# The last rows of a down projection, once by feature rows with seven-product sums, once by token rows

## The chip, the cores and the metric

The kernel runs on one core of a Trainium2 chip. The metric is the device time of one execution in microseconds (us); smaller is better. The engines are called as in the profile: PE (TensorE), DVE (VectorE), ACT (ScalarE), POOL (GpSimd) and SP (SyncE, which issues nearly all transfers).

## What is computed

One layer of a streaming encoder: norm, attention in two kinds of heads, output projection, residual, norm, SwiGLU FFN, residual, and a last norm. Only the end matters here. `x` has 576 tokens (512 of the prompt, 64 of the sample) of 2048 features; the FFN is 5632 wide.

```python
def rmsnorm(x, g):
    xf = x.astype(jnp.float32)
    y = xf * lax.rsqrt(jnp.mean(xf * xf, axis=-1, keepdims=True) + EPS)
    return (y * g.astype(jnp.float32)).astype(x.dtype)
...
    h = rmsnorm(x, lp['norm_ffn_g'])
    x = x + (jax.nn.silu(h @ lp['ffn_w_gate']) * (h @ lp['ffn_w_up'])) @ lp['ffn_w_down']
...
    y_prompt = rmsnorm(xp[:, N_META:], final_norm_g)
    y_sample = rmsnorm(xs, final_norm_g)
```

## The kernel before, in words

Activations lie with features on the partitions and tokens along the columns: a tile is 128 features x 576 tokens, used in two halves of 288 (`QH`). Every operand of a product is split into a high and a low part in a reduced format (`split`: ACT copies the high part, DVE subtracts it to get the low one), and a product is three matmuls: high x high, low x high, high x low. Nearly all instructions of DVE, ACT and SP are recorded by one helper, so the profile gives them line L125.

**Seven products.** FFN and down projection use `winograd`: four quarters of a 256 x 256 piece of weights and four of the activations are combined so that seven products do the work of eight. A product's weights are a raw quarter or a sum (`subtotal`, on POOL and DVE, tiles `ws`), split into `wh` and `wl`; its activations are the operand tiles `b1` to `b7` of a pair. A **pair** is 256 FFN features (two tiles), numbered `u` or `m`, 22 in all; operand tile `b{p}_{m % 8}` holds product p of pair m.

**FFN.** 44 turns: a gate turn and an up turn for each pair u, 168 matmuls each. The result of a pair is turned into its operands: the four quarters and four sums (POOL, L1770 to 1773), which `parts` splits on ACT and DVE into seven pieces and stores in `partspill` (288 KB each), one piece a step of the following turn. The first two pairs (`WHOLE`) and the last two are stored whole instead (`actspill`, `sumspill`). The last turn (`ending`, up turn of pair 21) already loads the operands of block 0 step by step (`starter`), two steps ahead of their use; whole ones are split in place. From the ending turn on SP's issues stand in program order, and DVE's and ACT's order is set by the scheduler except where `pin` fixes it.

**Down projection.** Blocks of pairs, `blocks = [4, 4, 4, 4, 4, 2]`. For each of the first five, eight passes d (256 output features each): raw weights are loaded (1024 KB), seven products of 12 matmuls follow (L1436 with `wh`, L1440 with `wl`), and `take` adds each product from PSUM to the running sums `y[i]` (16 tiles, features on partitions, residual included). While a block runs, `fetcher` loads the next one's operands from `partspill`, and before the last block `builder` loads and splits the quarters of pairs 20 and 21.

**The last block** (pairs 20 and 21, 512 weight rows) multiplies plainly: `plain_weights` loads and splits, `plain_rows` does mm3 (L193, 3 matmuls for each of 4 k-chunks, 288 columns), and after each, `squares` forms the square of the finished sum (ACT or POOL, L1831, L1836) and scales the sum by the last norm's gain (ACT). First all passes for token half 0, then for half 1. `finish` sums the squares over the partitions by a matmul with ones (L1863), turns the sums to token rows by transposes on PE (L1849, 96 tokens), scales them by the root on the way out of PSUM (DVE and ACT in turn) and stores them (28 stores).

## Time and profile before

| what | value |
|---|---|
| median of 3 runs | 2393.21 us (2392.88 to 2395.0) |
| profiled execution, its own time | 2394.53 us |
| its span, first to last instruction | 2392.8 us |
| mean granted clock of PE | 0.997 |
| PE busy | 2365.2 us, 99% |
| DVE, ACT, POOL busy | 1782.5, 1169.8, 718.0 us |
| last plain product to end of span | 2375.4 to 2392.8 |

The span is what the hardware profiler saw of one execution; the 1.7 us between it and that execution's time lie before the first or after the last instruction. Busy times of different engines overlap. A group of the trace gives the operation as tile written <- tiles read, with the shape; `SPq` is SP's issue of transfers.

### The profile page before, as it was taken

How to read it: one execution, taken by the hardware profiler on the slowest of the kernel's cores; microseconds unless marked ns; L12 is line 12 of the kernel's file. 1: busy time of each engine (PE TensorE's matmuls, PEld its weight loads, DVE VectorE, ACT ScalarE, POOL GpSimd, SP SyncE). 2: the span in 40 equal slices, each digit the busy share in tenths (PEclk: the TensorE clock that was granted, in tenths of full speed). 3: DMA queues.
4: the chain of work that ended last, by engine and by line, in shares of the span. 5: the costliest groups of instructions: out<-in, count | busy, mean ns of one | idle time of the engine just before them, and what ended most of it. 6: DMA issues, size and time to landing. Idle time of an engine off the chain costs nothing.

```text
span 2392.8 us, 44550 instructions
## 1 busy us (share of the span) xinstructions
PE 2365.2 (99%) x17580; PEld 2333.4 (98%) x17580; DVE 1782.5 (74%) x2823; ACT 1169.8 (49%) x2223; POOL 718.0 (30%) x568
## 2 busy tenths in 40 slices
PE   9999999999999999999999999999999999999998
PEld 8999999999999999999999999999999999999998
DVE  5665666676565788788888888888887887888873
ACT  5544445455454554455545555555545433333345
POOL 0000000020001454554454454454454322222223
PEclk9999999999999999999999999999999999999999
DMA  9423323353223553334434434434435964754332
GB/s 276 125 86 86 93 85 94 94 159 113 89 94 114 166 170 108 126 107 154 160 111 151 161 118 143 161 120 141 160 129 175 315 230 143 232 188 140 120 113 80
DMA packets 329266, 336.92 MB, mean 141 GB/s; under 512 B 22482, under 2 KB 273272, under 8 KB 329024
## 3 DMA queue, kind: packets, MB, share of 16 engines
q1 hardware_dynamic: 327520, 330.56, 42.7%
q0 software_dynamic: 1104, 3.22, 0.4%
q8 instruction: 138, 2.26, 0.4%
q14 instruction: 72, 0.59, 0.1%
q10 hardware_dynamic: 432, 0.29, 0.0%
HBM read 264.68 MB, written 72.68 MB: 141 GB/s over the span
## 4 chain that ended last, share of the span: by engine, by line
PE 59%; DVE 1%; DMA 0%; issue 0%; POOL 0%; ACT 0%; DVEq 0%; ACTq 0%; POOLq 0%; SPq 0%
PE m L1436 38%; PE m L1440 19%; PE m L193 2%; PE m L1849 0%; DVE wl L125 0%; DMA raw<-in_ffn_w_down 0%; DVE ws L125 0%; DMA b<-actspill 0%; POOL ws L1396 0%; DVE b L125 0%; PE m L1863 0%; DVE y L125 0%; ACT wh L125 0%; DVEq L2014 0%; DVE c L125 0%
## 5 line engine op out<-in xcount | busy, mean ns | idle before, releaser
L1436 PE MATMUL m<-b,wh 128*128 128x288 f32 x7168 | 1051.9, 296 | 2.7 <-DVE y L125 1.5
L1436 PEld LDWEIGHTS m<-b,wh 128*128 128x128 f32 x7168 | 983.2, 188 | 5.1 <-ACT wh L125 2.4
L1440 PE MATMUL m<-b,wl 128*128 128x288 f32 x3584 | 569.2, 294 | 1.9 <-DVE wl L125 1.8
L1396 POOL TENSOR_TENSOR ws<-raw 128x512 f32<-128x512 f32 (+1 forms) x258 | 364.8, 1423 | 539.6 <-DVE wl L125 277.7
L1440 PEld LDWEIGHTS m<-b,wl 128*128 128x128 f32 x3584 | 509.3, 188 | 3.3 <-DVE wl L125 3.3
L125 ACT ACTIVATE wh<-ws 128x512 fp32r<-128x512 f32 (+1 forms) x339 | 282.8, 845 | 392.0 <-PE m L1436 257.2
L125 DVE TENSOR_TENSOR wl<-ws,wh 128x512 fp32r<-128x512 f32 (+1 forms) x339 | 384.6, 1145 | 91.6 <-ACT wh L125 89.1
L125 DVE TENSOR_TENSOR wl<-raw,wh 128x512 fp32r<-128x512 f32 (+1 forms) x389 | 359.8, 949 | 10.2 <-ACT wh L125 9.6
L125 ACT ACTIVATE wh<-raw 128x512 fp32r<-128x512 f32 (+1 forms) x389 | 228.5, 620 | 283.8 <-PE m L1436 261.5
L108 PE MATMUL ps<-xh,wh 128*128 128x296 f32 (+1 forms) x960 | 217.6, 308 | 1.7 <-ACT wh L125 1.7
L108 PE MATMUL ps<-xl,wh 128*128 128x296 f32 (+1 forms) x960 | 208.5, 298 | 0.1
L125 DVE TENSOR_TENSOR y<-y,m 128x288 f32<-128x288 f32 x312 | 140.1, 450 | 90.0 <-PE m L1440 68.1
L108 PE MATMUL ps<-xh,wl 128*128 128x296 f32 (+1 forms) x928 | 202.1, 299 | 0.5 <-DVE wl L125 0.5
L125 DVE TENSOR_TENSOR ws<-ws,raw 128x512 f32<-128x512 f32 (+1 forms) x129 | 117.9, 920 | 58.5 <-POOL ws L1396 56.4
L108 PEld LDWEIGHTS ps<-xh,wh 128*128 128x128 f32 x960 | 155.4, 190 | 5.5 <-ACT wh L125 2.1
L108 PEld LDWEIGHTS ps<-xl,wh 128*128 128x128 f32 x960 | 155.8, 189 | 0.4 <-DVE xl L125 0.3
L108 PEld LDWEIGHTS ps<-xh,wl 128*128 128x128 f32 x928 | 151.0, 189 | 1.0 <-DVE wl L125 1.0
L125 DVE TENSOR_TENSOR wl<-wr,wh 128x1024 fp32r<-128x1024 f32 (+1 forms) x110 | 114.3, 1041 | 30.4 <-ACT wh L125 28.9
L125 ACT ACTIVATE wh<-wr 128x1024 fp32r<-128x1024 f32 (+1 forms) x112 | 99.8, 893 | 63.0 <-PE ps L108 36.2
L1651 POOL TENSOR_TENSOR c<-c,rb 128x576 f32<-128x576 f32 x42 | 67.2, 1599 | 168.8 <-ACT c L125 168.8
L703 POOL MEMSET bias<- 64x64 f32 x8 | 1.2, 144 | 365.3 <-DMA bias<-tsk 258.6
L1764 POOL TENSOR_TENSOR c<-c 128x576 f32<-128x576 f32 x42 | 73.7, 1754 | 87.3 <-DVE c L125 82.9
(420 smaller groups left out, 3109.0 us busy)
## 6 DMA issues: line engine op xcount, KB each, us to landing
raw<-in_ffn_w_gate SPq DMA_DIRECT2D x44, 1024.0 KB, 5.8
raw<-in_ffn_w_up SPq DMA_DIRECT2D x44, 1024.0 KB, 6.4
raw<-in_ffn_w_down SPq DMA_DIRECT2D x39, 1024.0 KB, 5.6
partspill<-parts SPq DMA_DIRECT2D x126, 288.0 KB, 2.1
b<-partspill SPq DMA_DIRECT2D x126, 288.0 KB, 6.2
wr<-in_w_in SPq DMA_DIRECT2D x54, 512.0 KB, 3.8
wr<-in_w_out SPq DMA_DIRECT2D x16, 512.0 KB, 4.0
wr<-in_w_out SPq DMA_DIRECT2D x28, 256.0 KB, 3.2
```

The source lines that it names most:

```text
L108: self.tc.keep_in_program_order(self.pe.matmul(out, lhsT, rhs, start=start, stop=stop))
L125: ins = issue(*args, **kwargs)
L193: PE.matmul(outs[i], w, x[i], start=start and p == 0, stop=stop and p == 2)
L703: G.memset(bias[0:64, 464:528], -BIG)
L1396: engine.tensor_tensor(w[:, k:k + m, :], pick(xs), pick(ys), op=op)
L1436: PE.matmul(banks[p], wh[:, k, :], x, start=first and new and k == 0 and x is hi, stop=False, skip_group_check=not new)
L1440: PE.matmul(banks[p], wl[:, k, :], hi, start=False, stop=last and k == n - 1, skip_group_check=not new)
L1651: engine.tensor_tensor(g[:, f, :], g[:, f, :], rb2, op=ALU.mult)
L1764: G.tensor_tensor(w[:, f, :], w[:, f, :], g[:, f, :], op=ALU.mult)
```

## The change

- `blocks = [4, 4, 4, 4, 5, 1]`: pair 20 becomes a fifth pair of block 4 (1280 weight rows by seven products), pair 21 alone is left for the last block. The fifth pair's raw weights and split weights lie in operand tiles that are free (`fifth_raws`, `fifth_tiles`), and its operands are loaded late in block 3 (`late_parts`).
- So pair 20 goes through `parts`: three pieces in the gate turn of pair 21 and four in the ending turn. In the ending turn the pieces follow the order of `CHAIN`. The raw weights of pass 1 of block 0 (`fetch_raw_in_halves`) are loaded in its fifth step, no longer ahead of it.
- During block 4 `turn(q)` transposes four finished sums at a time, by groups of 128 tokens (the last has 64), and ACT moves them out of PSUM (passes 3, 5, 7; the last quarter in the last block).
- The last block: `token_rows(g, d)` has 128 tokens of pair 21's activations as the stationary operand and 256 weight columns as the moving one, so the result has tokens on the partitions. After each odd pass DVE adds 512 columns from PSUM to the turned sums, ACT squares them with an accumulated sum per token, and POOL multiplies the first two quarters by the gain; after pass 7 the root is taken and the four pieces are scaled (two on ACT, two with the gain on DVE) and stored. Groups 0 and 1 run side by side over the passes, then groups 2, 3 and 4. `squares`, `finish` and the sums with ones are gone.

In the whole program PE has 17511 instructions in place of 17518: the 384 plain matmuls of 288 columns, 16 transposes and the sums with ones leave, 168 matmuls of 288 columns and 240 of 256 come.

```diff
+    def fifth_tiles():
+        if not fifths:
+            r = room(fifth_weights, F32R)[:, 0:4 * P].rearrange("p (k c) -> p k c", k=4)
+            fifths.extend([[r[:, 2 * i:2 * i + 1, :], r[:, 2 * i + 1:2 * i + 2, :]] for i in range(2)])
+        return fifths.pop()
...
     def split_weights(wpool, n, srcs):
+        if n == 5:
+            srcs = srcs if len(srcs) == 2 else [srcs[0][:, 0:4, :], srcs[0][:, 4:5, :]]
+            parts = [weight_tiles(wpool, 4), fifth_tiles()]
+            for (wh, wl), s in zip(parts, srcs):
+                split(wh, wl, s)
+            return [[x[i][:, k, :] for x in parts for k in range(x[i].shape[1])] for i in range(2)]
...
+    def late_parts(m):
+        for p, _ in CHAIN:
+            fetch_parts(m, p)
+            yield
...
-    blocks = [4, 4, 4, 4, 4, 2]
+    blocks = [4, 4, 4, 4, 5, 1]
...
             if ending:
                 Q.ordered = True
                 fetch_raw(0, blocks[0], 0)
-                fetch_raw_in_halves(0, blocks[0], 1)
...
                     try:
-                        pieces.send(took[WIDE[done[0] - 1][0]][:, 0:1])
+                        pieces.send(took[(chain or WIDE)[done[0] - 1][0]][:, 0:1])
...
                 if ending:
                     next(start)
+                    if done[0] == 5:
+                        fetch_raw_in_halves(0, blocks[0], 1)
...
+    def turn(q):
+
+        rooms = [columns[i] for i in range(4 * q - 4, 4 * q) if i in columns]
+        rooms += [room(names) for _ in range(5 - len(rooms))]
+        for g, t in enumerate(rooms):
+            o, n = groups[g]
+            ps = pmt()
             for k in range(4):
+                PE.transpose(ps[0:n, k * P:(k + 1) * P], column(4 * q + k, o, n), ident)
+            turned[g, q] = t[0:n, 0:512]
+            S.activation(turned[g, q], ps[0:n, :], AF.Copy)
+            yield
+
+    def token_rows(g, d):
+
+        o, n = groups[g]
+        if d % 2 == 0:
+            banks0[g] = pmt()
+        out = banks0[g][0:n, d % 2 * 256:d % 2 * 256 + 256]
+        for k, (hi, lo) in enumerate(acts):
+            wh, wl = kept[d][k]
+            for i, (a, b) in enumerate(((hi, wh), (hi, wl), (lo, wh))):
+                PE.matmul(out, a[:, o:o + n], b, start=k + i == 0, stop=k == len(acts) - 1 and i == 2)
+        q, fine = d // 2, g == 4 and d > 5
+        if d % 2 or fine:
+            cs = slice(d % 2 * 256, d % 2 * 256 + 256) if fine else slice(0, 512)
+            at = 8 * g + q + (d == 7 and fine)
+            z = turned[g, q][:, cs]
+            V.tensor_tensor(z, z, banks0[g][0:n, cs], op=ALU.add)
+            S.activation(junk[0:n, cs], z, AF.Square, accum_out=small[0:n, at:at + 1])
+            if q < 2:
+                G.tensor_tensor(z, z, gain[q][0:n], op=ALU.mult)
+        if d == KC // 2 - 1:
+            v, r = small[0:n, 48 + g:49 + g], small[0:n, 56 + g:57 + g]
+            V.tensor_reduce(v, small[0:n, 8 * g:8 * g + 4 + fine], axis=AX.X, op=ALU.add)
+            V.tensor_scalar(v, v, 1.0 / D, EPS, op0=ALU.mult, op1=ALU.add)
+            rsqrt(r, v)
+            for q in range(4):
+                z = turned[g, q]
+                if q < 2:
+                    S.activation(z, z, AF.Copy, scale=r)
+                else:
+                    V.scalar_tensor_tensor(z, z, r, gain[q][0:n], op0=ALU.mult, op1=ALU.mult)
+                cs = slice(q * 512, (q + 1) * 512)
+                store(y_prompt[o:o + n, cs] if g < 4 else y_sample[:, cs], z)
...
             for d in range(KC // 2):
+                if bi + 2 == len(blocks) and d in (3, 5, 7):
+                    turning = turn((d - 3) // 2)
...
+                if bi + 3 == len(blocks) and d == KC // 2 - 1:
+                    late = late_parts(first + n + 4)
...
+            turning = turn(3)
             for d in range(KC // 2):
                 plain_weights(first, n, d)
-                plain_rows(d, 0, slots)
-            before = finish(0, 0)
-            for d in range(KC // 2):
-                plain_rows(d, 1, slots)
...
+                for g in range(2):
+                    token_rows(g, d)
+                if d == 1:
+                    for _ in turning:
+                        pass
```

The scheduler makes three orders of it that the prediction speaks of. First SP's issues around the ending turn. `raw_21481` (before) and `raw_21499` (after) are pass 0's raw weights of block 0, the two pieces of 128x4x256 pass 1's; `b1_0` to `b1_3` are the first product's operands of the four pairs. Before:

```order
L125 DMA raw_21481<-in_ffn_w_down 128x8x256
L125 DMA raw_21483<-in_ffn_w_down 128x4x256
L125 DMA raw_21485<-in_ffn_w_down 128x4x256
L125 DMA y0_21487<-x2spill_66 128x576
L125 DMA b1_0_21521<-actspill_67 128x288
L125 DMA b1_1_21523<-actspill_67 128x288
L125 DMA b1_2_21525<-partspill_69 128x576
L125 DMA b1_3_21527<-partspill_69 128x576
```

After, two pieces of the same list:

```order
L125 DMA partspill_69<-parts_21487 128x576
L125 DMA b1_0_21540<-actspill_67 128x288
L125 DMA b1_1_21542<-actspill_67 128x288
L125 DMA b1_2_21544<-partspill_69 128x576
L125 DMA b1_3_21546<-partspill_69 128x576
L125 DMA partspill_69<-parts_21539 128x576
L125 DMA b5_0_21586<-sumspill_68 128x288
```

```order
L125 DMA b7_2_21731<-partspill_69 128x576
L125 DMA b7_3_21733<-partspill_69 128x576
L125 DMA raw_21739<-in_ffn_w_down 128x4x256
L125 DMA raw_21741<-in_ffn_w_down 128x4x256
L125 DMA b3_0_21776<-actspill_67 128x288
L125 DMA b3_1_21778<-actspill_67 128x288
L125 DMA b3_2_21780<-partspill_69 128x576
L125 DMA b3_3_21782<-partspill_69 128x576
```

A store of a piece of pair 20 now stands ahead of each step's loads, and pass 1's raw weights stand behind the fifth product's operands and ahead of the sixth's. Second, ACT in the same place: `b3` and `b4` are the operands of the sixth and seventh product, and after the change `wh_21960` takes the last quarter of pass 0 and, from the two raw pieces, the first quarter of pass 1. Before:

```order
L125 ACTIVATE b3_0_21739<-b3_0_21739 128x288
L125 ACTIVATE wh_21850<-ws_21848 128x512
L125 ACTIVATE b3_1_21741<-b3_1_21741 128x288
L125 ACTIVATE c_21480<-m_21489 128x288
L125 ACTIVATE wh_21850<-raw_21481 128x512
L125 ACTIVATE b4_0_21785<-b4_0_21785 128x288
L125 ACTIVATE b4_1_21787<-b4_1_21787 128x288
```

After:

```order
L125 ACTIVATE wh_21924<-ws_21943 128x512
L125 ACTIVATE wh_21960<-raw_21499 128x512
L125 ACTIVATE wh_21960<-raw_21739 128x256
L125 ACTIVATE wh_21960<-raw_21741 128x256
L125 ACTIVATE b3_0_21776<-b3_0_21776 128x288
L125 ACTIVATE b3_1_21778<-b3_1_21778 128x288
L125 ACTIVATE wh_22005<-ws_22002 128x512
L125 ACTIVATE b4_0_21822<-b4_0_21822 128x288
L125 ACTIVATE b4_1_21824<-b4_1_21824 128x288
```

The splits of those operands moved behind the weights of two later products, among them pass 1's raw rows. In the same place TensorE, which before takes the sixth product (`b3`) whole behind the fifth (`b7`), now has:

```order
L1454 MATMUL m_21841<-b7_2_21731,wl_21925 128x288
L1454 MATMUL m_21841<-b7_3_21733,wl_21925 128x288
L1450 MATMUL m_21983<-b1_0_21540,wh_21960 128x288
L1450 MATMUL m_21865<-b3_0_21776,wh_21924 128x288
L1450 MATMUL m_21983<-b1_0_21540,wh_21960 128x288
L1450 MATMUL m_21983<-b1_1_21542,wh_21960 128x288 x2
L1450 MATMUL m_21865<-b3_0_21776,wh_21924 128x288
L1450 MATMUL m_21865<-b3_1_21778,wh_21924 128x288
L1450 MATMUL m_21983<-b1_2_21544,wh_21960 128x288 x2
L1450 MATMUL m_21983<-b1_3_21546,wh_21960 128x288 x2
```

The sixth product is mixed with the first of pass 1 (`b1`, with `wh_21960`). Third, ACT's last rows. Before, six scalings follow the root; `gT` is the gain:

```order
L125 ACTIVATE b7_2_27857<-y15_22636 128x288
L125 ACTIVATE y15_22636<-y15_22636,gT_248 128x288
L125 ACTIVATE b1_3_27871<-b1_3_27871 128x3 x2
L125 ACTIVATE b6_7_27896<-m_27865,b1_3_27871 96x512
L125 ACTIVATE b7_7_27913<-m_27908,b1_3_27871 96x512
```

After, with `b3_5` the small values and `b6_5` the place for unused squares:

```order
L125 ACTIVATE b6_5_27590,b3_5_27589<-b5_6_27407 128x512
L125 ACTIVATE b6_5_27590,b3_5_27589<-y11_22401 128x512
L125 ACTIVATE b6_5_27590,b3_5_27589<-b2_6_26666 64x512
L125 ACTIVATE b3_5_27589<-b3_5_27589 128x1 x2
L125 ACTIVATE b6_5_27590,b3_5_27589<-b4_6_27037 64x512
L125 ACTIVATE b1_6_26665<-b1_6_26665,b3_5_27589 128x512
L125 ACTIVATE y234_21834<-y234_21834,b3_5_27589 128x512
L125 ACTIVATE b6_5_27590,b3_5_27589<-b6_6_27408 64x512
L125 ACTIVATE b6_5_27590,b3_5_27589<-b3_0_27637 64x256 x2
L125 ACTIVATE b3_5_27589<-b3_5_27589 64x1 x2
L125 ACTIVATE b2_6_26666<-b2_6_26666,b3_5_27589 64x512
L125 ACTIVATE b4_6_27037<-b4_6_27037,b3_5_27589 64x512
```

The squares of one group now stand between those, the root and the scalings of the group before.

## Rows read from the trace of the kernel before

**Rows 1.** The page, busy time of each engine, share of the span, instructions.

```profile
PE 2365.2 (99%) x17580; PEld 2333.4 (98%) x17580; DVE 1782.5 (74%) x2823; ACT 1169.8 (49%) x2223; POOL 718.0 (30%) x568
```

**Rows 2.** Timeline of PE, last block: start us, us, engine, line, operation, tile.

```profile
2318.16 28.76 PE L193 MATMUL m<-b,b 128*128 128x288 f32 x216
...
2351.25 1.04 PE L1849 MATMUL m<-ident,y 128*96 128x128 f32 x8
2352.04 3.42 PE L193 MATMUL m<-b,b 128*128 128x288 f32 x24
```

**Rows 3.** Timeline of PE, six matmuls of 256 columns in the attention.

```profile
563.21 0.40 PE L108 MATMUL pv<-mw,ch 128*128 128x256 f32 x2
...
563.92 0.42 PE L108 MATMUL ps<-mxh,wh 128*128 128x288 f32 x2
```

**Rows 4.** Timeline of all engines, tail.

```profile
2379.15 0.15 DVE L125 TENSOR_SCALAR b<-m 96x1 f32<-96x1 f32 x1 [0.93 <-PE m L1863]
2379.34 0.44 ACT L125 ACTIVATE b<-b 128x3 f32<-128x3 f32 x2 [2.41 <-DVE b L125]
...
2380.40 4.04 DVE L125 TENSOR_SCALAR b<-m,b 96x512 f32<-96x512 f32 x6
...
2381.16 8.35 SPq L125 DMA_DIRECT2D out<-b  x16
```

**Rows 5.** Groups of ACT by shape: count, busy us, mean ns, idle before.

```profile
L125 ACT ACTIVATE wh<-raw 128x512 fp32r<-128x512 f32 x383 | 226.5, 623 | 281.4 <-PE m L1436 259.0 <-DMA raw<-in_ffn_w_up 13.8 <-DVE wl L125 8.5
...
L125 ACT ACTIVATION_READ_ACCUMULATOR e<-e,nm 128x1 f32 x64 | 11.9, 187 | 0.0
...
L125 ACT ACTIVATE b<-m,b 96x512 f32<-96x512 f32 x12 | 7.7, 683 | 3.5 <-PE m L1849 2.8 <-DVE b L125 0.7
```

**Rows 6.** Groups of DVE by shape.

```profile
L125 DVE TENSOR_TENSOR parts<-c,parts 128x288 fp32r<-128x288 f32 x126 | 60.8, 483 | 0.0
...
L125 DVE COPY na<-pna 128x512 f32<-128x512 f32 x16 | 11.0, 688 | 5.7 <-PE pna L112 5.6
...
L125 DVE SCALAR_TENSOR_TENSOR sq<-sq,r 128x576 f32<-128x576 f32 x8 | 6.0, 756 | 0.2
```

**Rows 7.** Timeline of DVE, last block.

```profile
2321.05 0.69 DVE L125 TENSOR_TENSOR b<-raw,b 128x512 fp32r<-128x512 f32 x1 [0.62 <-ACT b L125]
...
2329.50 2.41 DVE L125 TENSOR_TENSOR b<-raw,b 128x512 fp32r<-128x512 f32 x2 [0.29 <-ACT b L125]
...
2342.19 0.45 DVE L125 TENSOR_TENSOR y<-y,m 128x288 f32<-128x288 f32 x1 [1.13 <-PE m L193]
```

**Rows 8.** Timeline of POOL, last block.

```profile
2330.22 1.14 POOL L1836 TENSOR_TENSOR b<-b,b 128x288 f32<-128x288 f32 x1
...
2342.04 0.80 POOL L1836 TENSOR_TENSOR b<-b,b 128x288 f32<-128x288 f32 x1 [0.17 <-ACT b L125]
```

**Rows 9.** Groups of POOL by shape.

```profile
L1396 POOL TENSOR_TENSOR ws<-raw 128x512 f32<-128x512 f32 x254 | 361.0, 1430 | 536.5 <-DVE wl L125 274.6 <-DMA raw<-in_ffn_w_down 135.6 <-ACT wh L125 42.9
```

**Rows 10.** Windows, seam and block 3: length, busy PE, PEld, DVE, ACT, POOL; clock, DMA.

```profile
1827.00:1849.50 22.50, 22.50 (x171) 22.50 (x171) 15.14 (x18) 9.85 (x15) 9.22 (x8) 1.00 0.52 167
1849.50:1872.00 22.50, 22.50 (x170) 22.27 (x168) 21.20 (x29) 13.90 (x30) 9.32 (x8) 1.00 0.94 303
1872.00:1883.00 11.00, 9.73 (x70) 9.36 (x71) 10.89 (x23) 3.68 (x8) 3.57 (x4) 1.00 1.00 351
...
1894.00:1905.00 11.00, 11.00 (x85) 11.00 (x84) 9.09 (x17) 3.46 (x6) 2.92 (x2) 1.00 0.74 256
2139.00:2217.00 78.00, 78.00 (x590) 78.00 (x589) 62.37 (x112) 28.83 (x50) 20.10 (x14) 1.00 0.52 173
```

**Rows 11.** Chain of waits in order of time, seam: start us, us, what.

```profile
1864.74 4.06 DMA b<-actspill
...
1872.90 1.30 PE m L1436 x8
```

**Rows 12.** Timeline of SP's DMA issues, ahead of the up turn.

```profile
1834.91 2.85 SPq L125 DMA_DIRECT2D raw<-in_ffn_w_down  x3
```

More of the change, by code (lines that the diff above doesn't have):

```diff
@@ L1369, in encoder_step @@
     spare = []
+    fifths = []
     def weight_tiles(wpool, n):
@@ L1386, in split_weights @@
             k += s.shape[1]
-        return wh, wl
+        return [[w[:, k, :] for k in range(n)] for w in (wh, wl)]
     def subtotal(spool, stag, n, engine, op, xs, ys):
@@ L1435, in winograd @@
                 for x in (hi, lo):
-                    PE.matmul(banks[p], wh[:, k, :], x, start=first and new and k == 0 and x is hi, stop=False,
+                    PE.matmul(banks[p], wh[k], x, start=first and new and k == 0 and x is hi, stop=False,
                               skip_group_check=not new)
@@ L1439, in winograd @@
                 hi, lo = operands[slots[k], p]
-                PE.matmul(banks[p], wl[:, k, :], hi, start=False, stop=last and k == n - 1,
+                PE.matmul(banks[p], wl[k], hi, start=False, stop=last and k == n - 1,
                           skip_group_check=not new)
@@ L1685, in fetch_raw_in_halves @@
             fetched[m0, d].append(r)
-    y = {}
+    y, columns = {}, {}
     def accumulator(i, tile):
-        y[i] = halves(tile)
+        y[i], columns[i] = halves(tile), tile
         load(tile, x2spill[i])
@@ L1784, in encoder_step @@
         store(actspill[FC - 2 + f], out["u"][:, f, :])
-    kept = {}
+    kept, turned = {}, {}
+    groups = [(o, min(P, TQ - o)) for o in range(0, TQ, P)]
     def plain_weights(m0, n, d):
         r = load_raw(fr, w_down, m0 * 256, 2 * n, d * 256, 2)
-        for f in range(2):
-            kept[d, f] = wh, wl = [room(names, F32R)[:, 0:4 * P].rearrange("p (k c) -> p k c", k=4) for _ in range(2)]
-            split(wh, wl, r[:, :, f * P:(f + 1) * P])
-    def plain_rows(d, h, slots):
-        for f in range(2):
-            wh, wl = kept[d, f]
-            out, c = pmt()[:, 0:QH], y[2 * d + f][h]
-            for k in range(4):
-                hi, lo = operands[slots[k // 2], ((1, 2), (4, 5))[k % 2][h]]
-                mm3([out], wh[:, k, :], wl[:, k, :], [hi], [lo], k == 0, k == 3)
-            V.tensor_tensor(c, c, out, op=ALU.add)
-            squares(2 * d + f, h)
+        kept[d] = []
+        for i in range(n):
+            w = [room(names, F32R)[:, 0:512].rearrange("p (k c) -> p k c", k=2) for _ in range(2)]
+            split(*w, r[:, 2 * i:2 * i + 2, :])
+            kept[d] += [[x[:, k, :] for x in w] for k in range(2)]
@@ L1815, in down_rows @@
         winograd(fw, fs, raws, slots, take, step=step, chain=CHAIN, made={5: sum5} if (m0, d) == (0, 0) else None)
-    tok = [[(h * QH + j * 96, 96) for j in range(3)] for h in range(2)]
-    sqs = [[], []]
     def room(names, dtype=F32):
         return bc.tile([P, 2, QH], dtype, name=next(names)).rearrange("p a b -> p (a b)")
-    def squares(i, h):
-        alone = i == 0 or h and i > KC - 4
-        t, c = room(names if alone else sums)[:, 0:QH], y[i][h]
-        if h or i % 2 == 0:
-            S.activation(t, c, AF.Square)
-        else:
-            G.tensor_tensor(t, c, c, op=ALU.mult)
-        S.activation(c, c, AF.Copy, scale=gE[:, i:i + 1])
-        if alone:
-            sqs[h].append(t)
-        else:
-            G.tensor_tensor(sqs[h][0], sqs[h][0], t, op=ALU.add)
@@ L1838, in finish @@
-    def finish(h, ahead):
-        groups = [(q, j) for q in range(4) for j in range(len(tok[h]))]
-        def turned(q, j):
-            o, n = tok[h][j]
-            ps = pmt()
-            for k in range(4):
-                PE.transpose(ps[0:n, k * P:(k + 1) * P], y[q * 4 + k][h][:, o - h * QH:o - h * QH + n], ident)
-            return ps
-        held = []
-        for g in groups[:ahead]:
-            held.append(turned(*g))
-            yield
-        pc = pmt()
-        small = room(names)
-        vc, rc = small[:, 0:len(tok[h])], small[:, 8:8 + len(tok[h])]
-        V.memset(vc, 1.0)
-        for j, (o, n) in enumerate(tok[h]):
-            at = o - h * QH
-            for i, t in enumerate(sqs[h]):
-                PE.matmul(pc[0:n, 2 * j:2 * j + 2], t[:, at:at + n], ones[:, 0:2],
-                          start=i == 0, stop=i == len(sqs[h]) - 1)
-            V.tensor_scalar(vc[0:n, j:j + 1], pc[0:n, 2 * j:2 * j + 1], 1.0 / D, EPS, op0=ALU.mult, op1=ALU.add)
-        rsqrt(rc, vc)
-        yield
-        for i, (q, j) in enumerate(groups):
-            o, n = tok[h][j]
-            ps = held.pop(0) if held else turned(q, j)
-            ot = room(rows[h])[:, 0:512]
-            if i % 2:
-                S.activation(ot[0:n], ps[0:n, :], AF.Copy, scale=rc[0:n, j:j + 1])
-            else:
-                V.tensor_scalar(ot[0:n], ps[0:n, :], rc[0:n, j:j + 1], None, op0=ALU.mult)
-            cs = slice(q * 512, (q + 1) * 512)
-            r = min(n, SEQ - o)
-            store(y_prompt[o:o + r, cs], ot[0:r])
-            if r < n:
-                store(y_sample[o + r - SEQ:o + n - SEQ, cs], ot[r:n])
-            yield
```

81 lines of the change are left out of this document (52 added, 29 removed).

## The prediction, before the changed kernel had run

> **What bounds the kernel now.** I began with the busy times of the page [rows 1]: TensorE works 2365.2 of 2392.8 us, every other engine far less. So the time is TensorE's list of matmuls, the few places where it stands still, and what follows its last matmul. The reader is to see there that a faster VectorE alone buys nothing, and that only three stretches matter here: the seam from the FFN into the down projection, block 4, and the last block with the tail. I then read these three: TensorE's own timeline of the last block [rows 2], a stretch with matmuls of the new width [rows 3], the timeline of the tail [rows 4], the groups of ScalarE and VectorE by shape [rows 5, 6], VectorE beside GpSimd [rows 7 to 9], and for the seam the windows, the chain of waits and SyncE's issues [rows 10 to 12].
>
> The profiled execution took 2394.5 us, 1.3 above the median of the three runs, 2393.2. I make the sum against the former and take 1.3 off at the end. A measurement of this kernel can tell a change of 0.2% (4.8 us) from none: faster is below 2388.4, slower above 2398.0.
>
> **Block 4 and the last block.** Before, the first plain product starts at 2318.16 and the span ends at 2392.8: 74.6 us. 216 matmuls of 288 columns take 28.76 us there, so 0.133 each; eight transposes start 0.79 us ahead of what follows them, so 0.099 each [rows 2]. The change takes away all 384 plain products, the transposes and the sums with ones. It adds:
> - the fifth pair of block 4: 168 matmuls x 0.133 = 22.4 us;
> - 60 transposes inside block 4: 60 x 0.099 = 5.9 us. The last block so starts 28.3 us after 2318.16;
> - 240 token matmuls of 256 columns. Six of that width stand between 563.21 and 563.92 [rows 3]: 0.118 each, 28.3 us. The nearest other rows bound this: 0.133 if they are no shorter than those of 288 columns (31.9 us), and 0.105 if a fixed part is smaller than I think (25.2);
> - 20 transposes of the last quarter, 2.0 us.
>
> TensorE's last matmul comes 30.3 us into the last block. What follows is set by ScalarE and VectorE. I walked through their two lists row by row, in order. ScalarE has in the last block 6 halves of a split x 0.62, 5 evictions of turned sums x 0.68, 19 squares of 512 x (0.62 + 0.19 for reading the accumulator out), two half squares of about 0.5, 10 scalings x 0.68 and five times 0.44 for the root [rows 4, 5]: 32.5 us. VectorE has 5 subtractions x 0.69, 19 additions from PSUM x 0.69 (the row of a copy from PSUM of that size), two halves x 0.45 at most, 10 scalings with the gain x 0.76 (the nearest row, of 576 columns) and some 25 one-column operations x 0.15 [rows 4, 6]: 29 us. Both are about as long as TensorE's 30.3, and each waits for the other at every group's end. The walk gives the last scaled output at 37.5, the last store's issue at 38.7, and the end 3.3 us later, as in the tail of before, where SyncE issues until 2381.16 + 8.35 = 2389.5 and the span ends at 2392.8 [rows 4]. So the last block takes 42.0 us, 28.3 + 42.0 = 70.3 against 74.6: **4.3 us gained**. The low end: if nothing lags, behind the last matmul stand only an addition (0.45 at most), a half square (0.5), the small operations up to the first scaled output (2379.15 to 2380.40, 1.25 [rows 4]), two scalings (1.4), half a microsecond of issues and the same 3.3, and the block takes 37.7, another 4.3 less.
>
> One thing must be added to the walk. It took VectorE's operations at the length they have alone. In the last block of before, a subtraction with both inputs in SBUF takes 0.69 us while GpSimd is idle, but two take 2.41 where GpSimd is squaring; the addition whose second input is in PSUM stays at 0.45 in the stretch where GpSimd squares without a pause [rows 7, 8]. After the change GpSimd multiplies 10 times by the gain (1.43 each, 14.3 us, a third of the block [rows 9]) beside 15 operations of that exposed kind (5 subtractions, 10 scalings). At 0.52 longer each (2.41 / 2 - 0.69) and a third of them hit this is 2.6 us, at most 7.8 if all are hit. ScalarE, not VectorE, is the longer list, so I take a third: **1.0 us lost**. The Trainium skill, page "SBUF — State Buffer", section "Who interferes with whom", says that a VectorE instruction with two SBUF inputs contends with a GpSimd instruction that reads SBUF, and one with a single SBUF input does not. By it none of the 21 additions is stretched and the 15 others can be; rows 7 agree in both halves (0.45 unchanged, 0.69 to 1.2).
>
> Block 4 itself: the small splits (9 subtractions of 128x128 per pass) come to VectorE, 62.4 of 78 us busy in such a stretch [rows 10]. By the slope between 0.45 at 288 columns and 0.69 at 512 they take 0.28 each, at most 0.45, and add 2.5 us, at most 4.1, to a pass that now takes 13.9 us in place of 11.2; its share is then 0.82, at most 0.94, and this lies beside TensorE. The extra raw rows (256 KB per pass) lie beside a DMA share of 0.52 [rows 10]. The fifth tile of weights is reused from product to product; at the block's start it waits once for the last product of block 3, for which I put **0.4 us**.
>
> **The seam.** Pair 20 now is split and stored in seven parts like the others: three in the gate turn of pair 21, where VectorE is busy 15.1 of 22.5 us and the DMA share 0.52, so free; four in the up turn, where VectorE is busy 21.2 of 22.5 and the DMA share is 0.94, and right behind which it is 1.00 at 351 GB/s [rows 10]. The raw rows of the second pass (2 x 512 KB) move from 1834.9 [rows 12] into this turn's fifth step. New there: 4 stores x 288 KB + 1024 KB, less two loads of block 1 (576 KB) now issued earlier: 1600 KB, 1.64 MB. At 351 GB/s that is 4.7 us; 6% of 22.5 us were free, 1.3. So what is queued behind comes 3.3 us later. It matters, because TensorE already loses 1.3 us here (9.73 of 11.00 [rows 10]): the chain goes from TensorE to a load of a block-0 operand, to its split on ScalarE and VectorE, and back [rows 11]. Four more subtractions x 0.48 on VectorE [rows 6] meet 1.3 us of room: 0.6. On ScalarE the split of the second pass's first weights, which needs the moved raw rows, now stands ahead of the operands of the sixth and seventh product; TensorE's order mixes the sixth product with the first of the second pass, 12 matmuls, 1.6 us, which can fill the gap. 3.3 + 0.6 - 1.6 = **2.3 us lost**. Bounds: 0, if the loads keep the lead that they have (from 1894 on the DMA share is 0.74, so the backlog is gone in the end); and 10 us: 6.2 if nothing of the 2.18 MB fits beside the old traffic, 0.6, and one step of 24 matmuls (3.2), as each step's loads stand on SyncE's list behind a store that waits for VectorE.
>
> **Sum.** 2394.5 - 4.3 + 1.0 + 0.4 + 2.3 = 2393.9, less 1.3: **2392.6 us**, no change that can be told.
>
> **The rivals.**
> - *The seam is hidden and the tail does not lag* (faster). For it: loads are issued two steps ahead, the filler product, and ScalarE's work can spread, as squares of groups 0 and 1 are done early. Against: TensorE waits in the seam already, and the two lists of the tail are as long as TensorE's. 2392.6 - 2.3 - 0.4 - 1.0 - 4.3 = 2384.6; half of the tail's part and no seam, 2387.2.
> - *The seam becomes a real stop* (slower). Loads of the first down products stand on one queue behind stores that wait for VectorE, in the stretch where VectorE and DMA are both full. The seam's full 10 us give 2392.6 + 7.7 = 2400.3. It decides from a seam loss of 7.7 us on. For it: DMA share 1.00 and the chain through the load [rows 10, 11]; against: before, a queue as full cost 1.3 us.
> - *The tail is bound by VectorE beside GpSimd*: all 15 operations stretched, 7.8 us in place of 1.0, half of it past ScalarE: 2392.6 + 3.4 = 2396.0, still no change that can be told. For it: the two that took 2.41 [rows 7]; against: GpSimd works a third of the time. This is what the rule of the Trainium skill's page "SBUF — State Buffer" (section "Who interferes with whom") would make of the time if every one of them met GpSimd.
> - *Token matmuls no shorter than those of 288 columns*: 3.6 us more on TensorE, of which the lagging tail hides about half: 2394.4.
>
> **How the numbers follow.** Forecast 0.31, the two mild rivals together 0.16: within 0.2%, 0.47. The faster rival 0.29, the slower one, alone or with a mild one on top, 0.24. The range goes from the faster rival's end, 2385, to the slower one's, 2400; beyond either is left about 0.1. No change to tell and its two mild rivals have a range of their own of 2389 to 2397.
>
> **What would show it.** In the profile after: token matmuls of 0.118 each and about 30 us from first to last; ScalarE and VectorE nearly without idle time in that stretch, and some 11 us from the last matmul to the end; a window behind the up turn in which TensorE is idle 3 to 4 us in place of 1.3, waiting for ScalarE or a load of an operand; block 4 longer than block 3 by 28 us and no new waits in it. I am wrong if TensorE stands still in the seam for 8 us or more, if it waits in the last block for weights, or if the end comes within 8 us of the last matmul.

## The result, and the profile after

The changed kernel is slower: 2399.2 us in the median of 20 runs, against 2395.6 of 20 runs of the kernel before that stood beside them; the ratio is 1.0015, with an interval of 1.0008 to 1.0021. That is 3.6 us, less than the 0.2% that the prediction called a change one can tell, but clear of zero with so many runs. The forecast was 2392.6, 0.6 us below the median of the three runs known then.

The profiled execution has a span of 2397.4 us (before 2392.8). The page's busy times first, the answer to [rows 1]:

```profile
PE 2361.5 (99%) x17558; PEld 2329.2 (97%) x17558; DVE 1810.2 (76%) x2886; ACT 1177.5 (49%) x2290; POOL 718.5 (30%) x563
```

TensorE works 3.7 us less than before and the span is 4.6 us longer, so 8 us more of it stand still. The timeline of PE in the last block (columns as in [rows 2]) shows where:

```profile
2349.47 3.03 PE L1851 MATMUL m<-b,b 128*128 128x256 f32 x24
2352.33 2.34 PE L1837 MATMUL m<-ident,y 128*128 128x128 f32 x20
2354.43 25.16 PE L1851 MATMUL m<-b,b 128*128 128x256 f32 x210
2387.32 1.54 PE L1851 MATMUL m<-b,b 128*64 128x256 f32 x6 [7.73 <-DVE b L125]
```

The token matmuls take 2.86 / 24 = 0.119 us each (the first row gives way to the second after 2.86) and run without a gap from 2354.43 on, as forecast. Then TensorE waits 7.7 us for VectorE, with six matmuls left, which take 1.54 us; at full clock they take 0.91 (the first experiment below). The windows (columns as in [rows 10]) give the mean granted clock of the tail, 0.59, so mostly the lower of its two levels (1.2 of 2.4 GHz) after TensorE had stood still; the two upper rows are the seam:

```profile
1849.50:1872.00 22.50, 22.50 (x172) 22.50 (x171) 20.74 (x32) 14.55 (x33) 9.21 (x7) 1.00 0.89 299
1872.00:1883.00 11.00, 8.68 (x64) 8.25 (x64) 9.39 (x19) 4.19 (x10) 4.89 (x5) 1.00 1.07 378
...
2380.00:2397.00 17.00, 1.54 (x6) 1.14 (x6) 9.13 (x20) 7.81 (x22) 2.48 (x2) 0.59 0.44 141
```

Before, the same two windows of the seam had 22.50 and 9.73 us of PE [rows 10]. The seam loses 1.3 us before and 2.3 now, at two places of PE's timeline:

```profile
1874.11 1.28 PE L1450 MATMUL m<-b,wh 128*128 128x288 f32 x8 [1.45 <-DVE y L125]
...
1880.64 1.44 PE L1450 MATMUL m<-b,wh 128*128 128x288 f32 x9 [0.87 <-DVE b L125]
```

How long each part took, by the timeline of PE: from the first product of the down projection to the last block 449.5 us before (1868.65 to 2318.16) and 480.2 after (1869.32 to 2349.47), 30.7 more where 31.0 were forecast. From the last block's first matmul to the end 74.6 before and 47.9 after, 4.9 more than the 43.0 forecast. **Nearly the whole miss is in the last block.** What happens there shows in the timeline of all engines:

```profile
2375.00 1.29 POOL L1860 TENSOR_TENSOR b<-b,b 128x512 f32<-128x512 f32 x1 [3.46 <-ACT b L125]
...
2375.29 1.02 DVE L125 TENSOR_TENSOR b<-b 128x1 f32<-128x1 f32 x1
...
2376.24 1.30 POOL L1860 TENSOR_TENSOR y<-y,b 128x512 f32<-128x512 f32 x1
2376.34 1.41 DVE L125 SCALAR_TENSOR_TENSOR b<-b 128x1 f32<-128x1 f32 x2
2377.79 1.42 DVE L125 SCALAR_TENSOR_TENSOR y<-y,b,b 128x512 f32<-128x512 f32 x2
2377.85 0.72 ACT L125 ACTIVATE b<-b,b 128x512 f32<-128x512 f32 x1 [1.95 <-DVE b L125]
...
2382.20 2.48 POOL L1860 TENSOR_TENSOR b<-b,b 64x512 f32<-64x512 f32 x2 [4.65 <-ACT b L125]
2382.49 1.00 DVE L125 TENSOR_TENSOR b<-b 128x1 f32<-128x1 f32 x1
...
2383.52 1.38 DVE L125 SCALAR_TENSOR_TENSOR b<-b 128x1 f32<-128x1 f32 x2
...
2384.99 0.72 ACT L125 ACTIVATE b<-b,b 128x512 f32<-128x512 f32 x1 [1.90 <-DVE b L125]
...
2386.26 1.00 DVE L125 TENSOR_TENSOR b<-b,m 64x512 f32<-64x512 f32 x2
...
2390.72 0.15 DVE L125 TENSOR_TENSOR b<-b 64x1 f32<-64x1 f32 x1 [0.50 <-ACT b L125]
2390.91 0.34 DVE L125 SCALAR_TENSOR_TENSOR b<-b 64x1 f32<-64x1 f32 x2
...
2392.09 2.43 SPq L125 DMA_DIRECT2D out<-b  x4
```

At 2375.29 VectorE begins an operation on one column, which takes 0.15 us when alone (the last group's, at 2390.72, when GpSimd is done). It takes 1.02 us and ends at 2376.31, just after GpSimd's multiplication, which began at 2375.00 and ended at 2376.29. The next two, together 0.34 us when alone (2390.91), take 1.41 beside GpSimd's second multiplication. Only then does ScalarE scale (2377.85, after 1.95 us of waiting). The next group repeats it (1.00 and 1.38 us, and 1.90 of waiting), and the additions that free banks for TensorE stand on VectorE's list behind all this: the two from 2386.26 on end at 2387.26, and TensorE goes on at 2387.32. By shape, in the whole last block:

```profile
L125 DVE SCALAR_TENSOR_TENSOR y<-y,b,b 128x512 f32<-128x512 f32 x7 | 7.0, 1038 | 0.4 <-DVE b L125 0.3
L125 DVE TENSOR_TENSOR b<-raw,b 128x512 fp32r<-128x512 f32 x5 | 4.6, 916 | 3.1 <-ACT b L125 1.9 <-PE m L1454 1.2
L125 DVE TENSOR_TENSOR b<-b,m 128x512 f32<-128x512 f32 x5 | 3.4, 683 | 0.9 <-PE m L1851 0.8
L125 DVE SCALAR_TENSOR_TENSOR b<-b 128x1 f32<-128x1 f32 x8 | 3.3, 418 | 0.2
L125 DVE TENSOR_TENSOR b<-b 128x1 f32<-128x1 f32 x4 | 2.3, 582 | 0.3
...
L125 DVE TENSOR_REDUCE b<-b 128x1 f32<-128x4 f32 x4 | 0.6, 155 | 1.0 <-ACT b L125 1.0
```

Over their length alone (0.75, 0.69, 0.16, 0.16) the first, second, fourth and fifth row have 2.0 + 1.1 + 2.1 + 1.7 = 6.9 us too much. The additions with one input in PSUM (0.68) and the reductions with one input (0.155) have none. The large ones that were held stand earlier in VectorE's timeline:

```profile
2359.63 1.82 DVE L125 TENSOR_TENSOR b<-raw,b 128x512 fp32r<-128x512 f32 x1
...
2366.32 2.49 DVE L125 SCALAR_TENSOR_TENSOR y<-y,b,b 128x512 f32<-128x512 f32 x2 [0.28 <-DVE b L125]
...
2370.38 2.38 DVE L125 SCALAR_TENSOR_TENSOR y<-y,b,b 128x512 f32<-128x512 f32 x2
```

Against their length without GpSimd (0.69 for the subtraction, 1.42 for a pair of scalings, as at 2377.79) they lose 1.1, 1.1 and 1.0 us; the four rows on one column above lose 0.9, 1.1, 0.9 and 1.0. So the 6.9 us are seven meetings of about 1 us each, whether the operation has one column or 512.

### The profile page after: what moved, and what is told of

The parts are those of the page before. It is cut to its first block, busy times and chain, and to the rows that moved or that the text cites. A ratio compares the mean times of both kernels' runs of the same rounds, so it can differ in the third digit from the quotient of the medians.

```text
span 2397.4 us, 44691 instructions
## 1 busy us (share of the span) xinstructions
PE 2361.5 (99%) x17558; PEld 2329.2 (97%) x17558; DVE 1810.2 (76%) x2886; ACT 1177.5 (49%) x2290; POOL 718.5 (30%) x563
## 5 line engine op out<-in xcount | busy, mean ns | idle before, releaser
L125 DVE TENSOR_TENSOR wl<-raw,wh 128x512 fp32r<-128x512 f32 (+1 forms) x389 | 366.3, 965 | 14.3 <-ACT wh L125 9.6
L125 DVE TENSOR_TENSOR y<-y,m 128x288 f32<-128x288 f32 (+1 forms) x291 | 133.0, 458 | 60.3 <-PE m L1454 58.1
L125 DVE TENSOR_TENSOR ws<-ws,raw 128x512 f32<-128x512 f32 (+1 forms) x129 | 111.6, 870 | 57.0 <-POOL ws L1410 54.7
L125 ACT ACTIVATE parts<-c 128x1 fp32r<-128x1 f32 (+1 forms) x266 | 85.7, 322 | 32.3 <-DVE c L125 26.3
```

What stands on the lines that cost most here:

```text
L125: ins = issue(*args, **kwargs)
```

## The experiments

The first two theories: **A**, GpSimd's ten multiplications hold up VectorE's operations with two inputs in SBUF, the tiny ones included, and these stand on the chain that ends last; **B**, VectorE and ScalarE wait for each other at each group's end whatever GpSimd does. The times before the seam differ by up to 6 us between executions (the down projection started between 1865.4 and 1871.5 us in the profiles), so the length of the last block, from its first token matmul to the end of the span, is compared inside each profile; the ratio, always to the kernel before, comes from the timed runs. Of the changed kernel they are 47.9 us and 1.0015. How far one profile can be trusted for this length: three versions below have the same last block (plain root; two of them change only the seam) and give 41.8, 41.8 and 42.0.

### GpSimd's multiplications left out

```diff
-            if q < 2:
-                G.tensor_tensor(z, z, gain[q][0:n], op=ALU.mult)
```

> The changed kernel without GpSimd's ten multiplications by the gain in the last block (the first 1024 output columns lack the last norm's gain). Theory A, the shared port: these ten stretch VectorE's operations with two SBUF inputs, and the chain runs through them; in the profile of the changed kernel the excess over their undisturbed length is 7 us between 2349.6 and the end (scalings 1.04 in place of 0.75, x7; one-column operations 0.42 to 0.58 in place of 0.16, x12; splits 0.92 in place of 0.69, x5). The last block then takes 42 to 44 us in place of 47.8, the time falls by 4 to 5 us against the changed kernel, to about 1 us below before. Rival B, the hand-overs: the lists of VectorE and ScalarE wait for each other at each group's end whatever GpSimd does; the last block stays at 46 to 48, the time within 1.5 us of the changed kernel.

Measured: 2392.4 us, ratio 0.9986 (0.9977 to 0.9995). Last block 41.4 us. PE's timeline and VectorE's groups:

```profile
2345.83 3.03 PE L1851 MATMUL m<-b,b 128*128 128x256 f32 x24
...
2377.76 0.91 PE L1851 MATMUL m<-b,b 128*64 128x256 f32 x6 [1.80 <-DVE b L125]
```

```profile
L125 DVE SCALAR_TENSOR_TENSOR y<-y,b,b 128x512 f32<-128x512 f32 x7 | 5.0, 748 | 0.4 <-DVE b L125 0.3
...
L125 DVE SCALAR_TENSOR_TENSOR b<-b 128x1 f32<-128x1 f32 x8 | 1.3, 158 | 0.2
...
L125 DVE TENSOR_TENSOR b<-b 128x1 f32<-128x1 f32 x4 | 0.6, 156 | 0.3
```

TensorE's wait falls from 7.7 to 1.8, the one-column operations are back at 0.16, and the six last matmuls take 0.91, at a granted clock of 1.00. VectorE's list in this block has the same operations in the same order as the changed kernel's, so no new order of it hides in the difference. A holds, B falls: 6.5 of the last block's 47.9 us hang on these ten instructions. The prediction's walk without GpSimd had given 42.0.

### The same work on GpSimd, for nothing

Leaving the multiplications out also takes a step out of the chain, as scalings had to wait for their result. So here GpSimd multiplies at the same points, but nobody uses the product:

```diff
             if q < 2:
-                G.tensor_tensor(z, z, gain[q][0:n], op=ALU.mult)
+                G.tensor_tensor(spent[0:n], gain[q][0:n], small[0:n, at:at + 1].to_broadcast([n, 512]), op=ALU.mult)
...
+                    spent = room(names)[:, 0:512]
```

> GpSimd again multiplies 128x512 ten times in the last block, at the same points (after each square), but into a place that nobody reads, from the gain and one column of the small values; the sums themselves are not multiplied (the first 1024 output columns lack the gain). So GpSimd reads SBUF as before, but nothing waits for its result. Theory A, the shared port: as slow as the changed kernel, the last block (from the first token matmul to the end) 46 to 48 us, one-column operations on VectorE at 0.4 us and more. Rival C, what counts is that scalings wait for GpSimd's result: like the kernel without the multiplications, 41 to 42 us.

Measured: ratio 1.0006 (0.9997 to 1.0016), last block 46.6 us, and in VectorE's groups:

```profile
L125 DVE SCALAR_TENSOR_TENSOR y<-y,b,b 128x512 f32<-128x512 f32 x7 | 6.5, 970 | 0.1
...
L125 DVE SCALAR_TENSOR_TENSOR b<-b 128x1 f32<-128x1 f32 x8 | 2.7, 340 | 0.2
...
L125 DVE TENSOR_TENSOR b<-b 128x1 f32<-128x1 f32 x4 | 2.0, 493 | 0.3 <-ACT b L125 0.2
```

The disturbance is back without any dependence, with multiplications of 1.08 us in place of 1.3 to 1.4: 5.2 of the 6.5 us. So most of it is GpSimd's work beside VectorE's, not the wait for a result. Whether the other 1.3 us are the wait or the longer multiplications was not parted.

### The root without its refinement

```diff
-            rsqrt(r, v)
+            S.activation(r, v, AF.Ln)
+            S.activation(r, r, AF.Exp, scale=-0.5)
```

> The root is taken by ScalarE's two operations alone; the three one-column operations of VectorE that refine it are left out in the last block (15 in all). Theory A: of these the stretched ones cost up to 1.4 us for the pair and 1.0 for the single one in four groups, 5.6 us in all, most of it on the chain: the last block is 3 to 5 us shorter. Rival B: only their own length and one hand-over a group, of which the last group's counts: 0.7 to 1.5 us shorter.

Measured: 2394.2 us, ratio 0.9991 (0.9982 to 0.9999); last block 41.8 us. This is 6.1 us less from leaving out fifteen operations of 0.15 us, 1.1 us more than A expected at most (5), with GpSimd at work as before. TensorE's wait is 5.0 us shorter (2.8), its six matmuls 0.6 (0.91), and the last group's own refinement, 0.5 us behind them, is gone. Which operations count most is so clear: the large ones are still stretched (scalings 1.01), and the table below says what that costs, 1.9 us. One thing comes with the edit: some of ScalarE's squares and scalings change places on its list. They do so in both versions with the plain root; what the new order is worth alone was not tried.

> Neither GpSimd's multiplications nor the refinement of the root in the last block (the first 1024 output columns lack the gain). Theory A: without GpSimd the three one-column operations cost only their own 0.5 us a group, so the last block is 0.5 to 1.5 us shorter than without the multiplications alone (41.4). If leaving the refinement out saves much for another reason (the hand-over between ScalarE and VectorE): 38 to 39.

Both edits together: ratio 0.9981 (0.9970 to 0.9991), last block 39.9 us, 1.5 less than without the multiplications alone, at the upper end of what A expected. The four lengths stand so:

| last block, us | refined root | plain root |
|---|---|---|
| with GpSimd's multiplications | 47.9 | 41.8 |
| without | 41.4 | 39.9 |

Neither edit is worth its 6 us alone: the multiplications cost 6.5 with the refinement and 1.9 without it, the refinement 6.1 with them and 1.5 without. 4.6 us belong to the meeting of the two. The timed ratios (1.0015, 0.9991, 0.9986, 0.9981) agree, but with intervals of about 0.001 either way they could not show it alone. The last experiment on this asks whether the refinement is dear in the kernel before, where GpSimd is idle in the tail:

> The kernel before, its root without the refinement (three one-column operations of VectorE in each half). GpSimd is idle in its tail, so only the second half's 0.55 us of them and nothing else can go: 0.3 to 1 us less, no change that can be told. If the refinement were dear by itself, as the 6 us that it saved in the changed kernel could suggest: 3 us or more less.

Measured on the kernel before, with the same edit in `finish`: ratio 1.0002 (0.9993 to 1.0011), no change. It is not.

### The gain elsewhere

All scalings on VectorE:

```diff
-                if q < 2:
-                    S.activation(z, z, AF.Copy, scale=r)
-                else:
+                if True:
                     V.scalar_tensor_tensor(z, z, r, gain[q][0:n], op0=ALU.mult, op1=ALU.mult)
```

with GpSimd's multiplication gone.

> All 20 scalings on VectorE with the gain in the same instruction, none on ScalarE, nothing on GpSimd; the output is whole. Theory A: VectorE's list gets 10 operations of 0.75 (7.5 us) and loses 7 us of stretching, ScalarE's loses 7 us; the last block takes 45 to 47, so 1 to 3 us less than the changed kernel. Rival B: VectorE's list is the path and gets 7.5 us longer; the last block takes 50 to 55.

Measured: ratio 0.9999 (0.9990 to 1.0008), last block 43.8 us, 4.1 less than the changed kernel, where A expected 1 to 3: ten more operations of 0.74 us on VectorE cost less than the ten multiplications on GpSimd and the ten scalings on ScalarE that they replace.

One of the two quarters moved to VectorE, in groups 0 to 3 and with the plain root:

```diff
-            if q < 2:
+            if q < 1 or q < 2 and g == 4:
                 G.tensor_tensor(z, z, gain[q][0:n], op=ALU.mult)
...
-                if q < 2:
+                if q < 1 or q < 2 and g == 4:
                     S.activation(z, z, AF.Copy, scale=r)
```

> Without the refinement of the root; in groups 0 to 3 only the first quarter goes over GpSimd and ScalarE, three quarters are scaled with the gain on VectorE; group 4 as in the changed kernel. The output is whole. Half the disturbance is left for four operations of 0.75 more on VectorE: if VectorE's length is what bounds (29 us alone, 27 without the refinement, 30 here), no gain against the version with two quarters (41.8); if it is the disturbance, 40 to 41, and some 2392 us, 3 below before.

Measured: ratio 1.0001 (0.9992 to 1.0010), last block 44.7 us, 2.9 more than with two quarters on GpSimd (41.8).

```profile
2348.42 3.03 PE L1851 MATMUL m<-b,b 128*128 128x256 f32 x24
...
2383.49 1.54 PE L1851 MATMUL m<-b,b 128*64 128x256 f32 x6 [4.94 <-DVE b L125]
```

TensorE waits 4.9 us for VectorE, 2.2 more than with two quarters. My hope for 40 to 41 was wrong. VectorE's length alone does not explain it: with all 20 scalings and the refinement on VectorE, and GpSimd idle, the block was shorter (43.8). In the timeline of the fourth group:

```profile
2378.91 2.99 POOL L1860 TENSOR_TENSOR b<-b,b 64x512 f32<-64x512 f32 x2 [4.12 <-ACT b L125]
...
2380.69 1.76 DVE L125 SCALAR_TENSOR_TENSOR b<-b,b,b 128x512 f32<-128x512 f32 x1
```

Three scalings, not two, now stand ahead of the addition that TensorE waits for, and one of them still meets GpSimd (1.76 in place of 0.75 us; 1.54 with two quarters). The group's work on VectorE also begins 1.1 us later in the block. So the longer list is a part of it; the rest was not parted.

The sums of the third and fourth quarter left in PSUM (on top of the version with earlier raw rows, below):

```diff
-            V.tensor_tensor(z, z, banks0[g][0:n, cs], op=ALU.add)
-            S.activation(junk[0:n, cs], z, AF.Square, accum_out=small[0:n, at:at + 1])
+            bank = banks0[g][0:n, cs]
+            t = z if q < 2 else bank
+            V.tensor_tensor(t, z, bank, op=ALU.add)
+            S.activation(junk[0:n, cs], t, AF.Square, accum_out=small[0:n, at:at + 1])
...
-                    V.scalar_tensor_tensor(z, z, r, gain[q][0:n], op0=ALU.mult, op1=ALU.mult)
+                    V.scalar_tensor_tensor(z, held[g, q], r, gain[q][0:n], op0=ALU.mult, op1=ALU.mult)
```

> As the version with the raw rows two steps earlier and no refinement of the root, but the third and fourth quarter's sums stay in PSUM: VectorE adds in place there, ScalarE squares from there, and the scaling with the gain has one input in PSUM and one in SBUF. The output is whole, GpSimd multiplies as before. Theory A (only operations with two SBUF inputs are stretched): these scalings take 0.75 in place of 1.01, the last block 40 to 41 us in place of 41.8, the time 1 us less. If what stretches is something else that GpSimd does to VectorE: scalings stay at 1.0. A risk: the banks are held longer, and TensorE waits for one.

Measured: ratio 0.9993 (0.9984 to 1.0002), last block 41.2 us, where 40 to 41 were expected. In VectorE's groups the scaling (now from `m`, a PSUM bank) is not stretched; the subtraction of a split, with both inputs in SBUF, still is:

```profile
L125 DVE TENSOR_TENSOR b<-raw,b 128x512 fp32r<-128x512 f32 x6 | 5.3, 877 | 2.9 <-ACT b L125 1.7 <-PE m L1454 1.2
L125 DVE SCALAR_TENSOR_TENSOR y<-m,b,b 128x512 f32<-128x512 f32 x7 | 5.0, 745 | 0.0
```

That confirms which operations are exposed. It gains 0.6 us of last block against the plain root alone and nothing in the time that can be told: TensorE waits 2.0 us for a bank that ScalarE still reads, the risk named ahead.

### One part alone, and the seam

Block 4 with five pairs and the seam of the change, but the one pair left multiplied plainly, with the old `squares` and `finish` (a part of the edit):

```diff
...
+            out, c = pmt()[:, 0:QH], y[2 * d + f][h]
+            for k, (hi, lo) in enumerate(acts):
+                wh, wl = kept[d][k]
+                mm3([out], wh[:, f * P:(f + 1) * P], wl[:, f * P:(f + 1) * P], [hi[:, h * QH:(h + 1) * QH]],
+                    [lo[:, h * QH:(h + 1) * QH]], k == 0, k == len(acts) - 1)
```

> One part alone: block 4 with five pairs, and the seam of the change, but the last block (one pair) multiplied plainly with features on the partitions, with squares, sums with ones, transposes and scalings as before; nothing is turned ahead. If the token rows are what costs: block 4 adds 22.4 us, the last block has 192 matmuls x 0.133 = 25.6 and some 6.4 of transposes between them, then the tail of 17.4 as before: 71.8 in place of 74.6, less the seam's 1.6, so 1 to 2 us below before. If the block of five pairs or the seam is what costs: as slow as the changed kernel or slower. A third way: with half the matmuls the squares (ScalarE 0.98 for each of 32) no longer keep up, and the last block takes 34 us and more ahead of its tail.

Measured: 2405.7 us, ratio 1.0038 (1.0026 to 1.0051). The third way of the three. PE's timeline:

```profile
2344.59 14.39 PE L193 MATMUL m<-b,b 128*128 128x288 f32 x108
2367.43 0.48 PE L1892 MATMUL m<-ones,b 128*96 128x2 f32 x2 [8.45 <-POOL b L1865]
```

108 products run through in 14.4 us, then TensorE waits 8.45 us for GpSimd's sum of squares, as half as many matmuls no longer cover it; in the 17.6 us behind the wait the granted clock is 0.81. The last block takes 60.5 us. So with the plain end the block of five pairs costs more than it saves, and this part alone is worse than the whole.

The seam, with the plain root, so that the last block is the calm one:

```diff
-                    if done[0] == 5:
+                    if done[0] == 3:
                         fetch_raw_in_halves(0, blocks[0], 1)
```

> Without the refinement of the root, and the raw weights of pass 1 loaded in the third step of the up turn, not the fifth. If their place is what the seam costs (TensorE idle 2.3 us there after the change, 1.3 before): idle 1.3 or less, and 1 us less from the start of the down projection to the last block (480.2 after the change). If the traffic itself costs (the DMA engines are full either way): 2 us and more idle, only at other products.

Measured: 2392.8 us against 2395.0 of before, ratio 0.9989 (0.9980 to 0.9998). PE's timeline in the seam:

```profile
1871.33 1.30 PE L1450 MATMUL m<-b,wh 128*128 128x288 f32 x8 [0.60 <-DVE y L125]
...
1875.59 0.53 PE L1450 MATMUL m<-b,wh 128*128 128x288 f32 x2 [0.36 <-DVE b L125]
1876.83 0.93 PE L1450 MATMUL m<-b,wh 128*128 128x288 f32 x5 [0.71 <-DVE b L125]
```

It waits 1.67 us there, between the two expectations (1.3 or less, 2 and more). The time from the first product of the down projection to the last block is 477.7, 2.5 us less than the changed kernel's 480.2. But the version with sums in PSUM, which has the same seam, waits 2.3 us at the same lines and takes 480.1, and the seven versions with the changed kernel's seam and block 4 lie between 479.0 and 480.7. So the place of these rows has no effect that can be told: against the version with the plain root alone (0.9991) nothing is gained for sure. With `== 1`:

> The raw weights of pass 1 in the first step of the up turn, else as the version with the third step (no refinement of the root). If their place is what the seam costs: TensorE idles 1.3 us or less in the seam, 0.5 less than with the third step. If the traffic costs: no less idle than 1.7.

Measured: 2406.3 us, ratio 1.0055 (1.0041 to 1.0068). SyncE's issues and TensorE's wait:

```profile
1856.57 13.58 SPq L125 DMA_DIRECT2D b<-partspill  x17
1871.55 0.93 SPq L125 DMA_DIRECT2D raw<-in_ffn_w_down  x2
```

```profile
1879.52 2.58 PE L1450 MATMUL m<-b,wh 128*128 128x288 f32 x8 [7.86 <-ACT b L125]
```

This is no clean test of the place. With the raw rows asked for so early, the scheduler put 15 loads of block 1's operands (288 KB each; SyncE waited 5.7 us in all for products of TensorE among them) ahead of the raw rows on SyncE's list, and the operands of the second product behind:

```order
L125 DMA b3_7_22880<-partspill_69 128x576
L125 DMA b4_5_22225<-partspill_69 128x576
L125 DMA raw_21548<-in_ffn_w_down 128x4x256
L125 DMA raw_21550<-in_ffn_w_down 128x4x256
L125 DMA partspill_69<-parts_21539 128x576
L125 DMA b5_0_21590<-sumspill_68 128x288
```

So the raw rows went out at 1871.55, 1.7 us later than in the changed kernel (1869.82), and TensorE stood still for 7.9 us, and for shorter times behind that. The window from 1865 to 1900 (columns as in [rows 10]) has 11.0 us of idle TensorE, 2.3 in the changed kernel, and a granted clock of 0.80:

```profile
1865.00:1900.00 35.00, 23.98 (x140) 21.34 (x139) 19.72 (x37) 10.99 (x26) 6.49 (x7) 0.80 1.00 344
```

This is what the slower rival described, loads of the first products behind waiting entries on one queue. It cost more than the rival's 10 us: from the first product to the last block 492.6, 12.5 more than with the plain root alone (480.0).

## Why the prediction was wrong

- **Matmuls and block 4** were right: 30.7 us more to the last block (31.0 forecast, the seam's 2.3 and 0.4 among them), 0.119 us for a token matmul (0.118; the lower bound of 0.105 rests on no row). The 0.4 for the fifth tile was not measured by itself.
- **The seam** was right in mechanism and too dear: 1.0 us more idle time, where 2.3 were forecast; TensorE took the first product of pass 1 as a filler, and waited in two places. The rest of the 30.7 us is 1 us more than forecast, so that the sum agrees is in part luck.
- **The walk through the last block** came out right in its total: 42.0 without GpSimd's disturbance, 41.4 measured when the multiplications were left out. That is no proof of its parts: it added up 32.5 us for ScalarE and 29 for VectorE, and both were busy less, 26.7 and 26.6 (busy time counts once where neighbouring instructions overlap in the records). The windows of the last block, the changed kernel and then the version without the multiplications:

```profile
2349.47:2397.40 47.93, 31.66 (x262) 31.01 (x260) 33.61 (x62) 26.77 (x71) 13.20 (x10) 0.85 0.36 121
```

```profile
2345.83:2387.20 41.37, 31.05 (x262) 30.54 (x260) 26.59 (x62) 26.68 (x71) 0.00 (x0) 0.91 0.41 141
```

- **The step that failed** is the term "ScalarE, not VectorE, is the longer list, so I take a third: 1.0 us lost". The mechanism was named, the term mis-sized: 6.5 us went with the multiplications, 5.2 of them shown to be the disturbance. Two things were wrong in it. It counted 15 exposed operations, all large, and for these its 2.6 us were nearly right (3.1). It passed over the one-column operations of the root, which have two SBUF inputs as well: 3.8 us more, up to seven times their own length. And it let a third through (0.9, taken as 1.0), because it took ScalarE's list for the longer one. It was not: with GpSimd at work VectorE is busy 33.6 us, ScalarE 26.8 (the rows above). More than that, place counts: the one-column operations stand between ScalarE's root and ScalarE's scalings, and ahead of VectorE's additions that free TensorE's banks, so a stop there delays all three engines. The 4.6 us of the two-by-two table are this meeting. Of the 6.5 us 0.6 are the six matmuls at the lower clock after the longer wait.
- In sum, the span misses by 5.2 us (4.6 up where 0.6 down was forecast): 4.9 in the last block (5.5 of this term, less 0.6 by which the walk was long), 0.3 less ahead of it, and 0.7 that this execution was late before the seam. The third rival had the mechanism, 3.4 us above the forecast, but it too counted the large operations alone. The prediction's own signs of being wrong did not show (the seam lost 2.3 us, TensorE waited for no weights, the end came 8.5 us after the last matmul); what it said of the right course failed: 39.4 us from the first to the last token matmul in place of 30.
- The Trainium skill, page "SBUF — State Buffer", section "Who interferes with whom", calls the port pair that VectorE and GpSimd share an exclusive lock, and says that issue order, not the operation's shape, decides who blocks. The one-column operation that began 0.29 us after GpSimd's and ended 0.02 us after it (2376.31 and 2376.29) agrees.
- **A faster version** exists: with the plain root and the raw rows two steps earlier the change is faster than both kernels, 0.9989 (0.9980 to 0.9998) of before, 0.1% and just clear of noise; of its two edits only the root's is shown to matter. The walk's low end (37.7) was not reached: 39.9 is the shortest last block seen, in a version that leaves out the gain on half of the columns.

## What to carry to other kernels

Before work is put on GpSimd beside a busy VectorE, list VectorE's operations with two SBUF inputs in that stretch, the smallest too, and ask which of them stand between two other engines: a stop cost about 1 us here, most of GpSimd's 1.3, whatever the length of the operation stopped. Price a term by where it stands on the chain, not by which engine's list is longer, and test a suspect by doing its work for nothing in place of leaving it out. Where matmuls get fewer, look at what they were covering: half as many plain products uncovered 8.45 us of squares.

## What was not expected of the hardware

A VectorE operation on 128x1 elements took up to 1.02 us beside a GpSimd multiplication, against 0.15 alone. Six matmuls of 256 columns took 1.54 us after a wait of 7.7 us (granted clock 0.50 while they ran) and 0.91 after one of 1.8 (1.00). And executions whose programs differ only behind it differed by up to 6 us in how late the down projection starts; seven with the same seam and block 4 took 479.0 to 480.7 us from there to the last block, so that a difference of 1 us in that stretch can't be read from single profiles.
